# Two attention loops written out in a fixed order on four engines, in a two-layer hybrid encoder

## The chip, the core and the metric

The kernel runs on one core of one Trainium2 chip. The core has a matrix engine (TensorE, PE in the profile, with its weight loads shown as PEld), a vector engine (VectorE, DVE), a scalar engine (ScalarE, ACT), a general engine (GpSimd, POOL) and an engine that here only issues transfers (SyncE, SP). Each engine takes its own instructions strictly in order; between engines they wait on semaphores. The metric is the device time of one execution in microseconds (us), lower is better. A result is the median of several executions; the profile is that of one more execution.

## The reference

The input is 512 tokens of 1024 numbers, all float32, laid out as a grid of 8 by 64. Two layers are computed, and each is `h = h + attention(rmsnorm(h))` followed by `h = h + mlp(rmsnorm(h))`; a last rmsnorm gives the output.

```python
# layer 0: two groups of heads beside each other, one input and one output projection
qa, ka, va, cq, ckv, kr = split(h @ w_in)
qa = axial_rope(rmsnorm(qa), row, col)        # A: 8 query heads, 2 key/value heads of 64
ka = axial_rope(rmsnorm(ka), row, col)
oa = softmax(qa @ ka.T / 8) @ va
qb = rmsnorm(cq) @ b_w_uq                     # B: 8 heads from latents of 384 and 256
kvb = rmsnorm(ckv) @ b_w_ukv                  # 64 plain + 32 rotary, the rotary key shared
ob = softmax([q_nope, rope(q_rope)] @ [k_nope, rope(kr)].T / sqrt(96)) @ vb
h = h + concat(oa, ob) @ w_out
# layer 1: 16 heads, each query sees a clamped window of 8 rows by 16 columns
h = h + softmax(q @ k_window.T / 8 + bias) @ v_window @ w_out
# after either: square of relu
h = h + relu(rmsnorm(h) @ w_up) ** 2 @ w_down # 1024 -> 4096 -> 1024
```

## The kernel before, in words

**Numbers.** Every float32 operand of a matrix product is kept as a pair: a rounded part `hi` (a copy on ACT into the type fp32r) and the rest `lo` (a subtract, mostly on DVE, some on POOL). A product is three matmuls, hi by hi, hi by lo and lo by hi (`mm3`, L425 to L428). So each piece of data costs a copy on ACT and a second half on DVE before PE can use all of it. `split` (L741 to L743) does this for activations, `chunk` (L172 to L204) for weights, which a transfer on SP brings in as `raw` first. `weights(i)` (L217) makes chunks two ahead of their use.

**Filler.** Products that are not urgent are generators. `Fill` (L391 on) holds a queue of them; `fill.run(us)` adds credit and emits groups of three matmuls until it is used up. A group is booked at `MM3` = 0.69 us. The attention loops call `step` after each unit of work and so put filler between the units.

**Layer 0.** After the first projections, the filler queue gets the latents of q and kv (cq, ckv), the rotary key (`rotary_key`), the scales of the latents (`latents`), and the q, k and v parts of B's first four heads (`projB(0)`). Then `attend` (L851 on) goes over 16 heads (A's eight, then B's two groups of four) and 4 blocks of 128 queries, 64 units in all. For a unit, `scores` (L892) makes the score matmuls (L895), a reduce on DVE that scales, writes the scores to memory and takes the least (L899), the exp on ACT with its sum (L901), the reciprocal on DVE (L902) and the norm by it on POOL (L903). `transpose` (L856) takes the unit three back: four PE transposes (L862), a copy on ACT (L864) and a subtract on DVE (L865). `values` (L870) follows for each two units (L875), and at a head's end the two halves of the accumulator are added (L884, L885). At unit 35 the filler queue gets the output projection of the first four head pairs and `projB(1)`. `step` runs 1.5 us of filler per unit.

A's queries for head pairs 1 to 3 are rotated inside the loop: `rope_q` starts eight transfers on SP for the swapped rows and a multiply by cos on POOL (L486), and also emits the multiply by sin on POOL (L487); `sum_q` (L545 on) adds both on DVE (L547), splits the result and lays it out with three transfers on SP. It is called two units after `rope_q`.

**Layer 1.** `attend_C` (L1233 on) goes over 16 heads of 4 units in three steps: scores of units 3 and 0 (L1248), then `second` (transposes, L1271, and evacuation, L1275 and L1276, of the head before), filler; `finish` (values) of the head before, scores of units 1 and 2, filler; first transposes of this head, filler. `weigh` (L1250 on) is reduce (L1254), exp (L1256), reciprocal (L1257) and norm on POOL (L1258). The filler is the q/k projection of the next head pair (`projC`) and the values' (`valuesC`). `projC` lays out keys by three transfers of 256 KB for each head pair, issued from POOL's queue (L1186 twice, then L1187, which waits until the lo and hi parts are made and for what it overwrites). `step` runs 3.4, 2.85 or 4.0 us of filler, by the head.

**What sets the order.** The program names the operations in the order of the code above, and a scheduler then decides the order on each engine by its own estimates. The MLPs, with seven products in place of eight for most blocks, are outside the change.

Of the kernel before, what the change touches and what calls it, by code (L numbers as in the profile page):

```python
# [18 lines left out]
P = 128  # L19
# [16 lines left out]
def encoder_kernel(ctx: ExitStack, tc: tile.TileContext, ins, out, dbg=None):  # L36
# [136 lines left out]
    def chunk(parts, nk, ncol, heads=None, eng=None, first=False):  # L173
# [13 lines left out]
        v = lambda t: t[:, 0:m].rearrange("p (k n) -> p k n", k=nk)  # L187
        if heads is None:
# [4 lines left out]
            (eng or DVE).tensor_tensor(lo_[:, 0:m], raw[:, 0:m], f32(hi[:, 0:m]), op=ALU.subtract)  # L193
        else:

            na, nb = heads
            hn = ncol // (na + nb)
            r4 = r3.rearrange("p k (h e) -> p k h e", h=hn)
            for e0, n, o in ((0, na, 0), (na, nb, hn * na)):
                z = [v(t)[:, :, o : o + hn * n].rearrange("p k (h e) -> p k h e", h=hn) for t in (hi, lo_)]  # L200
                src = r4[:, :, :, e0 : e0 + n]
                ACT.activation(z[0], src, AF.Copy)
                (eng or DVE).tensor_tensor(z[1], src, f32(z[0]), op=ALU.subtract)
        return v(hi), v(lo_)  # L204
# [5 lines left out]
    asked, ready = [], []  # L210
# [18 lines left out]
    def seven_chunk(w, k0, c0):  # L229
# [10 lines left out]
        DVE.tensor_tensor(lo[:, 0:896], raw[:, 128:1024], f32(hi[:, 0:896]), op=ALU.subtract)  # L240
        return hi, lo
# [154 lines left out]
    class Fill:  # L396
# [33 lines left out]
    def split_g(src, g, dst):  # L430

        ACT.activation(dst[:, 0, :], src, AF.Copy, scale=g)
        DVE.scalar_tensor_tensor(dst[:, 1, :], src, g, f32(dst[:, 0, :]), op0=ALU.mult, op1=ALU.subtract)
# [42 lines left out]
    def rope(src, cos, sin, mask, n=P, far=False):  # L476

        sh = scratch()
        if far:
            q = mask[0]  # L480
            for b in range(0, n, q):
                SP.dma_start(sh[b : b + q, :], src[b ^ q : (b ^ q) + q, :])
        else:
# [3 lines left out]
        (POOL if far else DVE).tensor_tensor(sh[0:n, :], sh[0:n, :], sin[0:n, :], op=ALU.mult)  # L487
        if far:
            return c, sh
        DVE.tensor_tensor(c[0:n, :], c[0:n, :], sh[0:n, :], op=ALU.add)  # L490
        return c

    def stats_to_tok(bk, n, name):

        st = scratch()
        ACT.activation(st[0:n, :], bk[0:n, :], AF.Copy)
        tb = stb()
# [45 lines left out]

    def sum_q(t):
# [5 lines left out]
        DVE.tensor_tensor(lo, rt, f32(q[:, 0, :]), op=ALU.subtract)  # L550
        SP.dma_start(f32(q[0:64, 1, :]), f32(q[64:128, 0, :]))
        SP.dma_start(f32(q[64:128, 1, :]), f32(lo[64:128, :]))
        SP.dma_start(f32(q[64:128, 0, :]), f32(lo[0:64, :]))
# [81 lines left out]
    def load_w(k):  # L635
        W[k] = chunk([(0, 768, rows(w_in, k, 1)[:, :, 0:768])], 1, 768, first=k == 0)
# [54 lines left out]
    def ev_kr(b):  # L691
        kc, kl = scratch(), scratch()
        ACT.activation(kl[0:32, :], b[32:64, :], AF.Copy)
        DVE.tensor_tensor(kc[0:32, :], b[0:32, :], kl[0:32, :], op=ALU.add)
        kr = rope(kc, cosB, sinB, sw8, 32)
        bk = stb()
        bcast_cols(lambda i: r0[:, i : i + 1].to_broadcast([P, 32]), 32, bk)
        DVE.tensor_tensor(kr[0:32, :], kr[0:32, :], bk[0:32, :], op=ALU.mult)
        kp = kst.pair()
        ACT.activation(kp[0:32, 0, :], kr[0:32, :], AF.Copy)  # L700
        DVE.tensor_tensor(kp[0:32, 1, :], kr[0:32, :], f32(kp[0:32, 0, :]), op=ALU.subtract)

    def rotary_key():
# [13 lines left out]
        w.free()  # L717
        ev_kr(b)

    def latents():  # L720

        b = stb()
        for z in range(2):
            PE.matmul(b[0:2, :], ind2(z), sqs[z].t[:, 0:512], start=z == 0, stop=z == 1)
        sB = stats_to_tok(b, 2, "rsB")
        for z in range(2):
            sqs[z].free()
        scB = keep([P, 4], F32, "scB")
        DVE.tensor_scalar(scB, sB[:, :, 0], -(96.0 ** -0.5), 1.0, op0=ALU.mult, op1=ALU.mult)
        bk = stb()  # L730
        bcast_cols(lambda i: sB[:, i, 1:2].to_broadcast([P, P]), P, bk)
        hold["skvb"] = Slot(F32)
        ACT.activation(hold["skvb"].t[:, 0:512], bk, AF.Copy)
        hold["sB"], hold["scB"] = sB, scB
        for s_ in X:
            s_.free()
        yield 1.5
# [3 lines left out]
    def split(src, dst):  # L741
        ACT.activation(dst[:, 0, :], src, AF.Copy)
        DVE.tensor_tensor(dst[:, 1, :], src, f32(dst[:, 0, :]), op=ALU.subtract)  # L743
# [3 lines left out]
    def projB(g, last):  # L747
# [5 lines left out]
        def q_part():  # L753
            CQ = [s_.pair() for s_ in cqS]
            banks = three(3)
            for m in (2, 0, 1):
                for k in range(3):
                    hi, lo = (z[:, k % 2, m * P : (m + 1) * P] for z in weights(iq[k // 2]))
                    mm3(banks[m], hi, lo, CQ[k][:, 0, :], CQ[k][:, 1, :], k == 0, k == 2)
                    yield MM3  # L760
                if m == 2:
                    qc = scratch()
                    ACT.activation(qc, banks[2], AF.Copy)
                    qr = rope(qc, cosB, sinB, sw8)
                    stg = Slot()
                    split(qr, stg.pair())
                else:
# [3 lines left out]
                    split(banks[m], qa)  # L771
                    SP.dma_start(f32(qb[0:64, :, :]), f32(qa[64:128, :, :]))
                    for e, q in enumerate((qa, qb)):
                        j = 2 * m + e
                        SP.dma_start(f32(q[64:96, :, :]), f32(stg.pair()[32 * j : 32 * j + 32, :, :]))
# [5 lines left out]
        def k_part():  # L781
            CK = [s_.pair() for s_ in ckS]
            banks = three(2)
            for m in range(2):
# [8 lines left out]
                split(kn, ka)  # L793
                SP.dma_start(f32(kb[0:64, :, :]), f32(ka[64:128, :, :]))
                for k_ in (ka, kb):
                    SP.dma_start(f32(k_[64:96, :, :]), f32(kst.pair()[0:32, :, :]))
# [5 lines left out]
        def v_part():  # L802
# [3 lines left out]
            for ip in range(2):  # L806
# [13 lines left out]
                for ii in range(2):  # L820
# [3 lines left out]
                    DVE.scalar_tensor_tensor(v[:, ii, :, 64:128], src, sB[:, i, 1:2], f32(v[:, ii, :, 0:64]),  # L824
                                             op0=ALU.mult, op1=ALU.subtract)
# [4 lines left out]
        fill.add(f"q{g}", q_part())  # L830
# [18 lines left out]
    O = []  # L849

    def attend(heads, step):  # L851
# [17 lines left out]
        def values(h, half, pt):  # L869
# [9 lines left out]
            if half:  # L879
                a = 64 * h["e"]  # L880
                if h["e"] == 0:
                    hold["pair"] = scratch()
                c = scratch()
                ACT.activation(c[0:64, :], o[64:128, :], AF.Copy)  # L884
                DVE.tensor_tensor(hold["pair"][a : a + 64, :], o[0:64, :], c[0:64, :], op=ALU.add)  # L885
                if h["e"]:
                    O.append(Slot())
                    split(hold["pair"], O[-1].pair())
                h["after"]()

        def scores(h, i):
# [9 lines left out]
            ACT.activation(p, p, AF.Exp, bias=t[:, 1:2], scale=-1.0, accum_out=t[:, 2:3])  # L901
            DVE.reciprocal(t[:, 3:4], t[:, 2:3])  # L902
            POOL.tensor_scalar(p, p, t[:, 3:4], 1.0, op0=ALU.mult, op1=ALU.mult)  # L903
            return p

        for h in heads:
            for i in range(4):
                ripe = list(late_v)
                p = scores(h, i)
                if len(late_t) == 3:  # L910
                    transpose(*late_t.pop(0))
                late_t.append((h, i, p))
                if ripe:
                    values(*late_v.pop(0))
                step(h, i)
        for x in late_t:
# [3 lines left out]
            fill.run(1.5)  # L920

    def heads_A():
        for h in range(8):
# [17 lines left out]
    def heads_B(g):  # L941
        fill.until(f"v{g}")
        Q, K, V = (QKV[g][z] for z in "QKV")
        vv = [s_.t.rearrange("p (i h e) -> p i h e", i=2, h=4) for s_ in V]
        for j in range(4):
# [12 lines left out]
            def after(j=j):  # L958
                if j == 3:
                    for s_ in V:  # L960
# [3 lines left out]
                       vlhs=lambda kt, j=j: vv[kt // 2][:, kt % 2, j, :])  # L964

    rate = {"A": 1.5, 0: 1.5, 1: 0.75}
# [8 lines left out]
    def step(h, i):  # L975
        n = count[0]
        count[0] += 1
        if n == 35:

            ok = [s_.pair() for s_ in O]  # L980
            assert len(ok) == 4
            out_proj(w_out, 0, ok, [0, 1, 2], "out")
            projB(1, True)
            out_proj(w_out, 0, ok, [3, 4, 5], "out")
# [540 lines left out]
```

## Time and profile before

| | us |
|---|---|
| median of 3 runs | 1211.41 |
| lowest and highest | 1211.27, 1213.22 |
| the profiled execution, its own time | 1211.92 |
| the span of its profile | 1210.0 |
| first loop, first score matmuls to last values | about 67 to 250 |
| second loop | about 652 to 839 |

The span goes from the first to the last instruction that the profile shows; 1.92 us of the execution lie around it. In the profile a line number is a line of the kernel before, busy times are sums over an engine's instructions, and the shown length of a matmul includes time in which the next one already runs. The granted clock (PEclk) is the share of TensorE's full speed. The two MLPs fill 264 to 640 and most of 840 to 1210 us.

### The profile page before, as it was taken

To read this page: it belongs to the slowest core of one execution; us is meant where nothing else is said; L and a number is where in the kernel's file an instruction comes from. 1 tells how busy PE (TensorE), PEld (TensorE's weight loads), DVE (VectorE), ACT (ScalarE), POOL (GpSimd) and SP (SyncE) were. 2 spreads that over 40 slices of the span, in tenths; PEclk is the share of its full clock that TensorE was granted. 3 is DMA by queue.
4 is the path that set the end of the run, shared out by engine and by line. 5 is a ranking of instruction groups with operands and counts; after the bars stand their busy time and mean duration, and the time that the engine had idled before them with its cause. 6 is when DMAs were issued, how large, how long until landed. Compare 5 with 4: busy or idle time off the path is not lost.

```text
span 1210.0 us, 18784 instructions
## 1 busy us (share of the span) xinstructions
PE 1182.8 (98%) x6804; PEld 1012.4 (84%) x6804; DVE 797.6 (66%) x1409; ACT 615.0 (51%) x1035; POOL 424.5 (35%) x543
## 2 busy tenths in 40 slices
PE   9998999999999999999999999999999999999997
PEld 8676888887899889898887988988778988988985
DVE  4587888878678337547565666666984753764764
ACT  5577676764346326336434555554463642451553
POOL 3256252205365146146002122321244803713800
PEclk9999999999999999999999999999999999999999
DMA  7223214212234214347435454443222341351432
GB/s 241 71 66 93 74 49 132 70 53 70 79 88 148 87 61 131 96 124 232 129 87 157 140 152 132 126 114 106 70 79 61 106 157 44 88 158 44 122 122 70
DMA packets 105853, 127.96 MB, mean 106 GB/s; under 512 B 8755, under 2 KB 77664, under 8 KB 105760
## 3 DMA queue, kind: packets, MB, share of 16 engines
q1 hardware_dynamic: 102832, 119.30, 33.4%
q0 software_dynamic: 2176, 6.31, 2.2%
q10 hardware_dynamic: 752, 1.15, 0.3%
q8 instruction: 54, 0.88, 0.3%
q14 instruction: 39, 0.32, 0.1%
HBM read 104.32 MB, written 6.29 MB: 91 GB/s over the span
## 4 chain that ended last, share of the span: by engine, by line
PE 81%; DVE 8%; ACT 3%; POOL 3%; issue 2%; DMA 1%; SPq 1%; DVEq 0%; POOLq 0%; ACTq 0%
PE mm L428 7%; PE mm L427 7%; PE mm L426 7%; PE s L428 2%; PE s L426 2%; PE s L427 2%; PE o L875 2%; PE s L895 2%; PE mm L316 2%; PE mm L314 2%; PE mm L315 2%; PE mm L1424 2%; PE mm L1425 2%; PE mm L1423 2%; PE t L862 2%
## 5 line engine op out<-in xcount | busy, mean ns | idle before, releaser
L193 DVE TENSOR_TENSOR wlo<-raw,whi 128x1024 fp32r<-128x1024 f32 (+2 forms) x133 | 157.4, 1185 | 156.5 <-ACT whi L192 153.3
L192 ACT ACTIVATE whi<-raw 128x1024 fp32r<-128x1024 f32 (+2 forms) x136 | 134.7, 993 | 172.0 <-PE o L427 38.7
L240 DVE TENSOR_TENSOR wlo<-raw,whi 128x896 fp32r<-128x896 f32 x104 | 129.7, 1247 | 107.2 <-ACT whi L239 105.7
L426 PE MATMUL mm<-a,whi 128*128 128x512 f32 x460 | 185.6, 406 | 0.1
L427 PE MATMUL mm<-a,whi 128*128 128x512 f32 x460 | 183.1, 398 | 0.1
L428 PE MATMUL mm<-a,wlo 128*128 128x512 f32 x460 | 182.0, 397 | 0.1
L239 ACT ACTIVATE whi<-raw 128x896 fp32r<-128x896 f32 x104 | 98.8, 950 | 161.6 <-POOL raw L236 27.7
L234 POOL TENSOR_TENSOR raw<-raw 128x128 f32<-128x128 f32 x104 | 60.0, 577 | 266.7 <-DMA raw<-in_ffn_w_up_dram 190.3
L428 PEld LDWEIGHTS mm<-a,wlo 128*128 128x128 f32 x460 | 86.6, 189 | 21.1 <-issue 1.7
L427 PEld LDWEIGHTS mm<-a,whi 128*128 128x128 f32 x460 | 87.1, 189 | 18.9 <-issue 1.7
L426 PEld LDWEIGHTS mm<-a,whi 128*128 128x128 f32 x460 | 86.8, 189 | 18.4 <-issue 1.0
L235 POOL TENSOR_TENSOR raw<-raw 128x256 f32<-128x256 f32 x104 | 95.3, 917 | 8.2
L236 POOL TENSOR_TENSOR raw<-raw 128x128 f32<-128x128 f32 x104 | 92.4, 888 | 8.1
L316 PE MATMUL mm<-a,wlo 128*128 128x256 f32 x280 | 79.3, 283 | 1.8 <-DVE wlo L240 1.6
L315 PE MATMUL mm<-a,whi 128*128 128x256 f32 x280 | 78.6, 281 | 0.0
L314 PE MATMUL mm<-a,whi 128*128 128x256 f32 x280 | 78.6, 281 | 0.0
L903 POOL TENSOR_SCALAR p<-p,ti 128x512 f32<-128x512 f32 x64 | 45.6, 714 | 89.3 <-DVE ti L902 79.5
L1258 POOL TENSOR_SCALAR p<-p,ti 128x256 f32<-128x256 f32 x64 | 37.1, 584 | 110.4 <-DVE ti L1257 103.8
L316 PEld LDWEIGHTS mm<-a,wlo 128*128 128x128 f32 x280 | 52.7, 188 | 3.0 <-DVE wlo L240 2.8
L314 PE MATMUL t<-a,whi 128*128 128x256 f32 x192 | 53.9, 281 | 0.0
L315 PE MATMUL t<-a,whi 128*128 128x256 f32 x192 | 53.8, 280 | 0.0
L316 PE MATMUL t<-a,wlo 128*128 128x256 f32 x192 | 53.8, 280 | 0.0
(318 smaller groups left out, 3186.4 us busy)
## 6 DMA issues: line engine op xcount, KB each, us to landing
raw<-in_ffn_w_down_dram SPq DMA_DIRECT2D x64, 512.0 KB
raw<-in_ffn_w_up_dram SPq DMA_DIRECT2D x104, 256.0 KB
raw<-in_od_w_qkv_dram SPq DMA_DIRECT2D x64, 128.0 KB
raw<-in_ffn_w_up_dram SPq DMA_DIRECT2D x12, 512.0 KB
a<-a POOLq DMA_DIRECT2D x24, 256.0 KB, 3.8
raw<-in_ev_w_in_dram SPq DMA_DIRECT2D x12, 384.0 KB
bias<-bx SPq DMA_DIRECT2D x16, 256.0 KB
raw<-in_od_w_qkv_dram SPq DMA_DIRECT2D x8, 512.0 KB
```

The lines of the kernel that those rows point to most:

```text
L192: ACT.activation(hi[:, 0:m], raw[:, 0:m], AF.Copy)
L193: (eng or DVE).tensor_tensor(lo_[:, 0:m], raw[:, 0:m], f32(hi[:, 0:m]), op=ALU.subtract)
L235: POOL.tensor_tensor(r[:, 4:6], r[:, 2:3].to_broadcast([P, 2, P]), r[:, 0:7:6], op=ALU.add)
L236: POOL.tensor_tensor(r[:, 7], r[:, 3], r[:, 5], op=ALU.subtract)
L239: ACT.activation(hi[:, 0:896], raw[:, 128:1024], AF.Copy)
L240: DVE.tensor_tensor(lo[:, 0:896], raw[:, 128:1024], f32(hi[:, 0:896]), op=ALU.subtract)
L314: PE.matmul(o, wh, x[:, 0], start=kp == 0 and z == 0, stop=False, skip_group_check=True)
L315: PE.matmul(o, wh, x[:, 1], start=False, stop=False, skip_group_check=True)
L316: PE.matmul(o, wl, x[:, 0], start=False, stop=kp == self.np - 1, skip_group_check=True)
L426: PE.matmul(o, wh, xh, start=first, stop=False)
L427: PE.matmul(o, wh, xl, start=False, stop=False)
L428: PE.matmul(o, wl, xh, start=False, stop=last)
```

## The change

Both loops are wrapped in `fixed_order()`, a region in which PE, ACT, DVE and POOL run in the order in which the program emits the instructions. SP is still scheduled. Filler of `LEAD` = 8.0 us is emitted first in each region. Inside a region:

- A unit's reciprocal and norm are emitted after the next unit's reduce (`norm(*last)`); the transposes three back come ahead of the exp. In the second loop the exps, the reciprocals and the norms of two units are put apart by parts of the filler.
- `soon` puts second halves off (lo subtracts, the add of the accumulator's halves in `fold`, the add of `rope`, and the transfers that depend on them); `catch_up` emits them in the next unit. `chunk` returns its lo subtract, and `give_low` emits it one chunk behind.
- Filler per unit is 1.15 us in the first loop; in the second 2.85 us a step, 3.6 from head 13, cut in parts of 0.4 and 0.6 in two of the three steps.
- The sin multiply of a rotary query goes into a step of its own (`sin_q`, third unit of the pair's first head) and `sum_q` two units later.
- `latents` becomes three pieces that run beside the q part of B's first group; heads of B wait for the k part and, when the values need it, the v part. At unit 35 `projB(1)` stands ahead of the whole output projection.
- The 24 key transfers of the second loop go to SP's queue, after the put-off subtract. The rotary rows of B's queries go to their places at the end of the q part.

The diff, cut to its core:

```diff
-            (eng or DVE).tensor_tensor(lo_[:, 0:m], raw[:, 0:m], f32(hi[:, 0:m]), op=ALU.subtract)
+            low(lo_[:, 0:m], raw[:, 0:m], hi[:, 0:m])
...
-    def weights(i):
-        while len(ready) < min(i + AHEAD + 1, len(asked)):
+    def weights(i, ahead=AHEAD):
+        while len(ready) < min(i + ahead + 1, len(asked)):
             make, spec = asked[len(ready)]
-            ready.append(make(*spec))
+            hi, lo, lows = make(*spec)
+            ready.append((hi, lo))
+            low_parts.append(lows)
+
+            give_low(len(ready) - fixed[0])
+        give_low(i + 1)
         return ready[i]
+    put_off = []
+
+    def soon(z):
+        if fixed[0]:
+            put_off.append(z)
+        else:
+            z()
+
+    def catch_up():
+        todo, put_off[:] = list(put_off), []
+        for z in todo:
+            z()
...
     def split(src, dst, then=lambda: None):
+        def low():
+            DVE.tensor_tensor(dst[:, 1, :], src, f32(dst[:, 0, :]), op=ALU.subtract)
+            then()
+
         ACT.activation(dst[:, 0, :], src, AF.Copy)
-        DVE.tensor_tensor(dst[:, 1, :], src, f32(dst[:, 0, :]), op=ALU.subtract)
+        soon(low)
...
+    def fixed_order():
+        return tc.manual_schedule(engines={mybir.EngineType.PE, mybir.EngineType.Activation, mybir.EngineType.DVE,
+                                           mybir.EngineType.Pool})
...
         for h in heads:
             for i in range(4):
                 ripe = list(late_v)
-                p = scores(h, i)
+                p, t = scores(h, i)
+                if last:
+                    norm(*last)
+                catch_up()
                 if len(late_t) == 3:
                     transpose(*late_t.pop(0))
+                ACT.activation(p, p, AF.Exp, bias=t[:, 1:2], scale=-1.0, accum_out=t[:, 2:3])
+                last = p, t
                 late_t.append((h, i, p))
                 if ripe:
                     values(*late_v.pop(0))
                 step(h, i)
...
-                if e == 0 and t < 3 and i == 2:
-                    sum_q(t + 1)
+                if t < 3 and (e, i) in ((0, 2), (1, 0)):
+                    if e:
+                        sum_q(t + 1)
+                    else:
+                        sin_q()
...
-        fill.run(1.5)
+        fill.run(1.15)
...
-    attend(all_heads(), step)
-    fill.until("out")
+    with fixed_order():
+        fixed[0] = 1
+        fill.run(LEAD)
+        attend(all_heads(), step)
+        fill.until("out")
+        finish_off()
+        give_low(len(ready))
+        fixed[0] = 0
...
-                split(n_, ka)
-                for z in range(2):
-                    POOL.dma_start(f32(kb[64 * z : 64 * z + 64, :, :]), f32(ka[64:128, :, :]))
-                POOL.dma_start(f32(ka[64:128, :, :]), f32(ka[0:64, :, :]))
+                def lay_out():
+                    for z in range(2):
+                        SP.dma_start(f32(kb[64 * z : 64 * z + 64, :, :]), f32(ka[64:128, :, :]))
+                    SP.dma_start(f32(ka[64:128, :, :]), f32(ka[0:64, :, :]))
+
+                split(n_, ka, lay_out)
...
-            scores(h, (3, 0))
+            w = scores(h, (3, 0))
+            catch_up()
             if late[0]:
                 second(late[0])
-            step(n, 0)
+            for x in w:
+                weigh(*x)
+            step(n, 0, 0.4)
+            for x in w:
+                norm(*x)
+            step(n, 0, 0.6)
...
-        fill.run(3.4 if n < 4 else 2.85 if n < 13 else 4.0)
+        fill.run((2.85 if n < 13 else 3.6) * part)
```

More of the change, by code (lines that the diff above doesn't have):

```diff
@@ L202, in chunk @@
                 ACT.activation(z[0], src, AF.Copy)
-                (eng or DVE).tensor_tensor(z[1], src, f32(z[0]), op=ALU.subtract)
-        return v(hi), v(lo_)
+                low(z[1], src, z[0])
+        return v(hi), v(lo_), lows
     def rows(w, k0, nk):
         return w[k0 * P : (k0 + nk) * P, :].rearrange("(k p) n -> p k n", p=P)
-    asked, ready = [], []
+    asked, ready, low_parts = [], [], []
     AHEAD = 2
@@ L486, in rope, with add @@
         POOL.tensor_tensor(c[0:n, :], src[0:n, :], cos[0:n, :], op=ALU.mult)
[L487 to L490, printed above, removed]
+        DVE.tensor_tensor(sh[0:n, :], sh[0:n, :], sin[0:n, :], op=ALU.mult)
+        def add():
+            DVE.tensor_tensor(c[0:n, :], c[0:n, :], sh[0:n, :], op=ALU.add)
+            if then:
+                then(c)
+        soon(add)
         return c
@@ L693, in ev_kr, with add, end @@
         ACT.activation(kl[0:32, :], b[32:64, :], AF.Copy)
[L694 to L701, printed above, removed]
+        def add():
+            DVE.tensor_tensor(kc[0:32, :], b[0:32, :], kl[0:32, :], op=ALU.add)
+            rope(kc, cosB, sinB, sw8, 32, then=end)
+        def end(kr):
+            bk = stb()
+            bcast_cols(lambda i: r0[:, i : i + 1].to_broadcast([P, 32]), 32, bk)
+            DVE.tensor_tensor(kr[0:32, :], kr[0:32, :], bk[0:32, :], op=ALU.mult)
+            kp = kst.pair()
+            ACT.activation(kp[0:32, 0, :], kr[0:32, :], AF.Copy)
+            soon(lambda: DVE.tensor_tensor(kp[0:32, 1, :], kr[0:32, :], f32(kp[0:32, 0, :]), op=ALU.subtract))
+        soon(add)
     def rotary_key():
@@ L828, in v_part @@
                     s_.free()
-        fill.add(f"q{g}", q_part())
+        fill.add(f"q{g}", q_part() if last else beside(q_part(), latents()))
         fill.add(f"k{g}", k_part())
@@ L879, in values @@
             if half:
[L880 to L888, printed above, removed]
+                fold(o, h["e"])
                 h["after"]()
@@ L915, in attend @@
                 step(h, i)
+        norm(*last)
         for x in late_t:
@@ L1350, in encoder_kernel, with step @@
     w_out1 = ins["od_w_out"][0]
-    def step(n, z):
-        if n == 13 and z == 0:
+    def step(n, z, part):
+        if n == 13 and z == 0 and part < 0.5:
+            finish_off()
             for s_ in X:
@@ L1359, in step @@
                 out_proj(w_out1, 0, ok, cols, "out")
-        fill.run(3.4 if n < 4 else 2.85 if n < 13 else 4.0)
-    attend_C(step)
-    fill.until("out")
+        fill.run((2.85 if n < 13 else 3.6) * part)
+    with fixed_order():
+        fixed[0] = 1
+        fill.run(LEAD)
+        attend_C(step)
+        fill.until("out")
+        finish_off()
+        give_low(len(ready))
+        fixed[0] = 0
     ok = [s_.pair() for s_ in O[6:]]
```

220 lines of the change are left out of this document (142 added, 78 removed).

## The prediction

> **What bounds the kernel now.** I read the page's busy line first, then the busy time of each engine by stretches of the span, then the chain of waits inside the stretches where TensorE (PE) is not full.
>
> ```profile
> span 1210.0 us, 18784 instructions
> PE 1182.8 (98%) x6804; PEld 1012.4 (84%) x6804; DVE 797.6 (66%) x1409; ACT 615.0 (51%) x1035; POOL 424.5 (35%) x543
> ```
>
> PE is the bound of the whole, and the change gives it the same matmuls. Only time in which PE waits can be won: 1210.0 - 1182.8 = 27.2 us by this line. The next view splits it. Columns: from:to, length, then busy us of PE, PEld, DVE, ACT, POOL, and the granted PE clock.
>
> ```profile
> 48.00:68.00 20.00, 19.42 (x77) 11.45 (x76) 13.26 (x35) 11.40 (x22) 3.86 (x3) 1.00 0.32 83
> 68.00:115.00 47.00, 41.89 (x235) 33.39 (x234) 36.06 (x95) 37.53 (x82) 31.64 (x35) 1.00 0.27 76
> 115.00:160.00 45.00, 44.48 (x246) 34.92 (x247) 39.04 (x100) 29.82 (x65) 14.77 (x18) 0.96 0.30 73
> 160.00:250.00 90.00, 89.72 (x531) 75.58 (x530) 76.15 (x174) 62.46 (x132) 29.07 (x39) 1.00 0.29 81
> 250.00:264.00 14.00, 14.00 (x62) 11.18 (x62) 11.12 (x16) 8.84 (x13) 0.00 (x0) 1.00 0.14 39
> 650.00:690.00 40.00, 37.59 (x247) 32.96 (x246) 25.88 (x74) 22.39 (x54) 11.43 (x22) 1.00 0.55 153
> 690.00:810.00 120.00, 116.89 (x722) 102.75 (x721) 77.33 (x209) 66.82 (x151) 31.99 (x56) 1.00 0.49 132
> 810.00:840.00 30.00, 29.78 (x156) 24.82 (x155) 18.41 (x45) 14.09 (x31) 4.90 (x8) 1.00 0.39 111
> ```
>
> Two loops are in reach: the first (48 to 250 us, 64 units of one head and 128 queries) and the second (650 to 840, 16 heads of 4 units). PE is idle for 0.58 + 5.11 + 0.52 + 0.28 = 6.5 us in the first and 2.41 + 3.11 + 0.22 = 5.7 us in the second. That is a floor, because a matmul's shown length is longer than its turn:
>
> ```profile
> 48.62 0.39 PE L428 MATMUL mm<-a,wlo 128*128 128x512 f32 x1
> 48.85 0.40 PE L426 MATMUL mm<-a,whi 128*128 128x512 f32 x1
> ...
> 51.37 0.43 DVE L577 COPY sc<-rsA 128x512 f32<-128x512 f32 x1
> ...
> 51.85 0.33 PE L454 MATMUL t<-cst,sc 128*128 128x128 f32 x1
> ```
>
> The two starts are 0.23 us apart and each lasts 0.40, so the first 0.17 us of any stall leaves no idle time. If each of 64 units hides one such stall, the first loop loses up to 64 x 0.17 = 11 us more, and the second, in 48 steps, up to 8 us (an estimate from that overlap). Now the large gaps, from finer stretches:
>
> ```profile
> 64.00:68.00 4.00, 3.45 (x15) 2.52 (x14) 3.13 (x10) 1.78 (x3) 1.29 (x1) 1.00 0.27 77
> 96.00:100.00 4.00, 2.55 (x16) 1.96 (x16) 3.94 (x11) 3.90 (x9) 1.72 (x2) 1.00 0.43 116
> 112.00:116.00 4.00, 1.43 (x9) 1.06 (x9) 2.22 (x5) 2.36 (x6) 2.44 (x3) 0.97 0.00 0
> 116.00:120.00 4.00, 3.93 (x15) 2.44 (x15) 3.70 (x8) 2.98 (x7) 1.97 (x2) 0.61 0.76 180
> 650.00:654.00 4.00, 2.42 (x15) 1.87 (x14) 2.54 (x5) 1.74 (x3) 0.00 (x0) 1.00 0.64 166
> 700.00:704.00 4.00, 2.40 (x12) 1.68 (x11) 3.73 (x9) 2.63 (x7) 1.86 (x1) 1.00 0.35 101
> ```
>
> The gap of 2.57 us at 112 is paid twice: in the next 4 us the clock is 0.61, which loses 4 x 0.39 = 1.56 us. The chain names its cause:
>
> ```profile
> 107.99 3.27 DMA raw<-in_ev_b_w_uq_dram
> 111.26 1.27 POOL a L621
> 112.53 1.23 POOL sc L487
> ...
> 115.19 1.01 PE o L875 x5
> ```
>
> A weight load queued on SP behind eight rotary copies holds POOL; the rotary multiply L487 (sin) follows on POOL, a DVE add waits for that, and the lo half that the values matmuls (L875) need sits behind the add.
>
> **The change, part by part.** The written order puts sin one or two units ahead of the add that needs it and sends filler of 1.15 us instead of 1.5 us per unit, so that it lasts to the end.
>
> *Entry of the first loop, +3.4 us.* The written region is emitted behind everything before it, so on PE only one filler group (three matmuls) now stands ahead of the transposes L454, where five stood. Their input, the copy L577, does not come earlier: it ends at 51.80. The group's third matmul is the one at 48.62, its turn ends at 48.85, and PE starts again at 51.85: 3.0 us idle, with every later matmul behind it. From that I take the 0.55 us of idle at 64:68, which the 8 us of filler (12 groups of 0.69) put ahead of the first scores covers: +2.4. For the clock, the gap at 112 says up to 1.56 us behind a gap of this size; PE would also wait part of that time for a bank that ACT empties, so I take +1.0. Bounds 0 and +4.0.
>
> The Trainium skill, page "TensorE: Matmul & The Clock Gate", section "What's actually happening", says that the clock halves after an idle window of about 3.4 us. By that neither gap would suffice and the clock term is nothing (total 1202.5); the row at 116:120 speaks against it, and the row decides.
>
> *Units 0 to 19 (68 to 120 us), -7.8 us.* The sin multiply no longer precedes the subtracts of its own unit, and second halves go one unit later, behind the reduce. The waits at 96, 100 to 104 and 112 have their inputs a unit earlier. All idle of 68:115 goes, 5.1, with the clock loss, 1.56 and 4 x 0.03 = 0.12, and about six hidden starts of 0.17, 1.0: -7.8. Bounds -7.8 and 0. What is late next is the reciprocal, which waits one unit for its exp and so finds it done.
>
> *Units 20 to 34, +3.0 us.* Here DVE is nearly full: 39.04 of 45 us. Filler falls by 0.35 us a unit, so 15 units give PE 5.3 us less cover while DVE keeps its work (rotary key, latents, the splits of q and k): 45 - 5.3 = 39.7 us of PE against 39.04 of DVE that must now go in one fixed order with its waits. Bounds 0 (DVE is ahead by its slack of units 0 to 19) and +5.3 (all the missing cover shows as idle). I take +3.0, nearer to the upper end, since a 39.04 of 39.7 leaves no room for a wait.
>
> *Units 35 to 63, -2.0 us.* 160:250 shows 0.28 idle and up to 29 x 0.17 = 4.9 hidden; the 35 x 0.35 = 12 us of filler kept back comes into units that had none. Bounds -5.2 and 0. The rotary q copies of the second head group go to the end of their part on SP and its heads wait for k instead of v: nothing, since 160:250 shows no wait on them, and a late one would cost its landing, 3.27 us by the row at 107.99. At the exit nothing: 250:264 is full at 14.00, and the next products interleave as before.
>
> First loop: 3.4 - 7.8 + 3.0 - 2.0 = -3.4 us.
>
> *Second loop, entry and K, -1.5 us.* The chain there:
>
> ```profile
> 652.63 1.16 PE s L1248 x8
> ...
> 660.31 3.83 DMA a<-a
> ...
> 664.69 3.04 DMA a<-a
> ```
>
> K is laid out by three 256 KB copies a head pair, the third after the first has landed. Twelve filler groups (8 us) before the first scores cover the wait at 650:654 (1.58 us); its K still needs two transfers of some 3.8 us in a row, about 8 us, so I take 1.0 of it, and 0.5 of 656 to 668. Bounds -2.5 and 0. All 24 copies move from POOL to SP:
>
> ```profile
> POOL a L1186 <- DVE a L743: 85.0, 4, 77.4
> POOL a L1187 <- DMA a<-a: 21.9, 7, 4.8
> ```
>
> (waits in us: total, times, longest). POOL loses those waits; SP gains eight of up to 4.8 us, and the weight, bias and Q loads queue behind them. Weights are asked two chunks ahead and a pair's copies come once in two heads, so I take 0; the other end is that all seven waits, 21.9 us, pass on to PE.
>
> *Second loop, steps, -3.5 us.* The large gap at 700:704:
>
> ```profile
> 701.04 0.49 ACT L1256 ACTIVATE p<-p,ti 128x256 f32<-128x256 f32 x1
> ...
> 701.44 0.18 ACT L1256 ACTIVATION_READ_ACCUMULATOR p<-p,ti 128x1 f32 x1
> ...
> 701.81 0.16 DVE L1257 RECIPROCAL ti<-ti 128x1 f32<-128x1 f32 x1
> 701.89 1.21 DVE L193 TENSOR_TENSOR wlo<-raw,whi 128x1024 fp32r<-128x1024 f32 x1
> ...
> 702.14 2.34 POOL L1258 TENSOR_SCALAR p<-p,ti 128x256 f32<-128x256 f32 x2 [4.71 <-DVE ti L1257]
> ...
> 704.08 0.33 PE L1271 MATMUL t<-cst,p 128*128 128x128 f32 x1 [1.68 <-POOL p L1258]
> ```
>
> and, in the chain of waits,
>
> ```profile
> 702.14 1.89 POOL p L1258
> ```
>
> The two norms on POOL took 2.34 us, the first 1.89, so the second 0.45; the first ran beside the 1.21 us weight subtract. In the changed order the weight subtracts of nearly all heads stand behind both reciprocals and behind the evacuation that follows. The idle of 690:840, 3.33, goes but for 0.3; 2.0 of the 8 hidden goes; +1.5 comes in head 0, where a subtract of 1.21 us does stand ahead of the reciprocals: -3.5. Bounds -11 and +1.5.
>
> Sum: 1211.92 - 3.4 - 1.5 - 3.5 = **1203.5 us** against the profiled execution's own time (span 1210.0 plus 1.92 around it, which stays). The median of the runs lies 0.5 lower, 1211.41; I forecast 1203.
>
> **Rivals.**
>
> *Slower: the norm late in the second loop, 1217.* From the reduce's end to the transposes: exp 0.49 + 0.18, reciprocal 0.16, norm 0.45, three hand-overs of 0.1: 1.6 us for one unit, covered by 2.85 us of filler. A weight subtract ahead of the reciprocal (1.21) and one beside the norm (1.89 - 0.45 = 1.44) make it 4.2, late by 1.4. Where a weight chunk ends on that step, taken as 7 of 16 heads, that is 7 x 1.4 = 10 us, and the steps win nothing: 1211.9 - 3.4 - 1.5 + 10 = 1217. It decides from four heads on (5.6 us against the 4.9 won elsewhere). For it: the row of 1.89. Against it: the order named above.
>
> The Trainium skill, page "GPSIMD Engine Reference", section "1. Specifications", has POOL share its memory interface with VectorE and contend with instructions of two SBUF inputs. The trace agrees: 1.89 us beside such a subtract, 0.45 without.
>
> *No change in the first loop, 1208.* DVE becomes the bound of units 20 to 34 (+5.3), the clock drops in full (+1.56), the end wins nothing: 2.4 + 1.6 - 7.8 + 5.3 = +1.5, and the second loop -5.0: 1211.9 + 1.5 - 5.0. For it: 39.04 of 45. Against it: DVE comes with slack out of units 0 to 19, 36.06 of 47.
>
> *All the lost time comes back, 1194.* Entry 2.4 without the clock, -7.8, 0, -3.5 makes -8.9; the second loop 5.7 visible and 3 hidden, -8.7. Against it: the fixed order cannot fill a gap with what is ready.
>
> *It does not do what it says, 1211.* SP stays scheduled, and its late loads set the order anyway.
>
> **How the numbers follow.** Forecast (1197 to 1207) 0.46; slower rival 0.16; no change in the first loop (1207 to 1212) 0.19; all back 0.13; not what it says 0.06. Within 0.2% (2.4 us) is about what a measurement of this kernel cannot tell from no change. Faster by more, under 1209: 0.46 + 0.13 + half of 0.19 = 0.68; within: half of 0.19, less a little, and 0.06 = 0.14; slower 0.18. The range reaches from the all-back case to the slower rival's lesser half: 1193 to 1216.
>
> **What would show it.** Right: PE waits about 3 us near 49 with a clock under 1 soon after; no gap over 1 us from 68 to 120; small gaps at 125 to 160; the wait at 650 under 1 us; POOL norms all near 0.45 in the second loop. Wrong: SP copies waiting while weight loads arrive late, norms of over 1 us before transposes, or DVE over 95% in 120 to 160 with PE waiting on it.

## The result, and the profile after

The changed kernel takes 1259.44 us (median of 4 runs, 1257.84 to 1260.36) against 1212.24 before: a ratio of 1.0388, 95% interval 1.037 to 1.0406. It is 47 us slower where 8 us faster was forecast, and far outside the range.

The busy line of the page after the change, with its span:

```profile
span 1256.8 us, 18733 instructions
PE 1195.1 (95%) x6804; PEld 1018.2 (81%) x6804; DVE 798.7 (64%) x1409; ACT 615.3 (49%) x1035; POOL 412.3 (33%) x519
```

The span is 46.8 us longer. PE is idle for 1256.8 - 1195.1 = 61.7 us in place of 27.2, so 34.5 us are new waits. The other 12.3 us are longer matmuls: the same 6804 are busy for 1195.1 us in place of 1182.8. The granted clock is 0.986 over the whole in place of 0.995. The busy time of DVE and ACT is the same to 1.1 us, and POOL's is 12.2 us lower. So no engine got more to do.

Where it was lost shows in the stretches (columns as before: busy PE, PEld, DVE, ACT, POOL, clock):

```profile
48.00:68.00 20.00, 16.96 (x61) 9.13 (x60) 12.68 (x39) 11.69 (x21) 2.55 (x2) 0.91 0.26 66
68.00:115.00 47.00, 41.79 (x233) 34.42 (x231) 34.36 (x82) 34.49 (x75) 29.24 (x31) 1.00 0.28 74
115.00:160.00 45.00, 37.17 (x188) 27.84 (x189) 32.06 (x82) 22.50 (x47) 16.34 (x18) 0.89 0.23 54
160.00:250.00 90.00, 76.31 (x426) 62.68 (x425) 62.91 (x147) 54.50 (x119) 26.11 (x34) 0.96 0.24 66
...
676.00:700.00 24.00, 19.23 (x95) 15.52 (x93) 9.67 (x29) 8.46 (x20) 2.79 (x6) 1.00 0.54 133
700.00:800.00 100.00, 97.04 (x621) 85.88 (x620) 63.88 (x174) 55.52 (x128) 19.79 (x34) 1.00 0.52 142
800.00:850.00 50.00, 41.07 (x242) 34.92 (x242) 25.86 (x75) 22.54 (x56) 6.57 (x14) 0.90 0.36 97
```

From 115 to 160 us PE falls from 44.48 to 37.17 busy, and DVE from 39.04 to 32.06, ACT from 29.82 to 22.50 with it. Three engines are idle more at the same time. That points to a chain of waits, and not to a full engine. The first score matmul of the second loop starts at 683.0 us in place of 652.6, and its last one at 875.6 in place of 830.1:

```profile
L1386 PE MATMUL s<-a,a x128: 274/281/561, 683.0 to 875.6; 128*128 128x256 f32 x128
```

```profile
L1248 PE MATMUL s<-a,a x128: 276/281/387, 652.6 to 830.1; 128*128 128x256 f32 x128
```

So 30.4 us are lost up to the second loop, 15.1 more in it, and 1.3 after it.

What PE waits for in the first loop (us in total, times, longest), from the view of waits after the change:

```profile
PE o L990 <- DVE a L980: 5.8, 11, 1.2
PE mm L781 <- DVE a L777: 3.8, 1, 3.8
PE mm L466 <- POOL wlo L191: 3.5, 3, 2.1
PE mm L464 <- ACT whi L207: 3.2, 1, 3.2
PE t L977 <- DVE a L980: 2.2, 1, 2.2
PE t L802 <- DVE a L980: 2.1, 1, 2.1
PE t L977 <- DVE sc L763: 2.0, 1, 2.0
```

There is no one cause. The first row is eleven short waits of the values for their lo halves. The others are one wait each, three for L466, and most are 2 to 4 us long. They are for different things: the rotary key's weight (L781), the second latent projection's weight (L464, L466), and one of the two result banks `t` that DVE has not yet read. That last wait holds the sums for the latents' scales (L802) and the transposes (L977), behind a unit's subtract (L980) or the rotary key (L763).

The longest single wait, in the timeline:

```profile
107.32 4.99 SPq L522 DMA_DIRECT2D sc<-a  x8
...
112.41 0.52 SPq L775 DMA_DIRECT2D sc<-in_ev_w_in_dram  x1
...
115.03 0.42 ACT L776 ACTIVATE a<-sc 128x256 fp32r<-128x256 f32 x1 [1.39 <-DMA sc<-in_ev_w_in_dram]
115.48 0.43 DVE L777 TENSOR_TENSOR a<-sc,a 128x256 fp32r<-128x256 f32 x1 [1.05 <-ACT a L776]
115.97 1.54 PE L781 MATMUL mm<-a,a 128*64 128x512 f32 x3 [3.76 <-DVE a L777]
```

The eight rotary copies take SP 4.99 us to issue, and the weight of the rotary key stands behind them in SP's queue. Before the change the same eight copies held another load and PE lost 2.57 us at the same time of the run. The wait did not go; it now holds another operation, and at 3.76 us it is longer.

### The profile page after: what moved, and what is told of

The parts are those of the page before. It is cut to its first block, busy times and chain, and to the rows that moved or that the text cites. A ratio compares the mean times of both kernels' runs of the same rounds, so it can differ in the third digit from the quotient of the medians.

```text
span 1256.8 us, 18733 instructions
## 1 busy us (share of the span) xinstructions
PE 1195.1 (95%) x6804; PEld 1018.2 (81%) x6804; DVE 798.7 (64%) x1409; ACT 615.3 (49%) x1035; POOL 412.3 (33%) x519
## 3 DMA queue, kind: packets, MB, share of 16 engines
q10 hardware_dynamic: 752, 1.15, 0.3%
## 5 line engine op out<-in xcount | busy, mean ns | idle before, releaser
L464 PE MATMUL mm<-a,whi 128*128 128x512 f32 x460 | 188.3, 411 | 8.3 <-ACT whi L207 3.2
L466 PE MATMUL mm<-a,wlo 128*128 128x512 f32 x460 | 184.0, 401 | 6.1 <-POOL wlo L191 3.5
L466 PEld LDWEIGHTS mm<-a,wlo 128*128 128x128 f32 x460 | 87.5, 190 | 30.7 <-POOL wlo L191 4.8
L464 PEld LDWEIGHTS mm<-a,whi 128*128 128x128 f32 x460 | 87.6, 191 | 29.6 <-issue 5.5
L979 ACT ACTIVATE a<-t 128x512 fp32r<-128x512 f32 x64 | 37.9, 594 | 43.2 <-PE t L977 41.3
```

Source lines behind the costliest of these rows:

```text
L464: PE.matmul(o, wh, xh, start=first, stop=False)
L466: PE.matmul(o, wl, xh, start=False, stop=last)
```

## The experiments

Every kernel below is the changed one with the edit shown. Theory 1 was that the fixed order costs: in it an engine that comes to a late input stands, with ready work behind it. Theory 2 was that the other edits cost.

**Which loop.** The regions are taken away from both loops, from the second, or from the first:

```diff
-    with fixed_order():
+    with ExitStack():
```

> The changed kernel with every edit, but both loops left to the scheduler. Theory 1 (the fixed order itself costs: an engine stands still at a late input with ready work behind it): most of the 47 us comes back, 1205 to 1220. Theory 2 (the other edits cost: filler of 1.15, second halves put off, key copies on SP): it stays above 1245. Theory 1's chance as I see it: 0.7.

> The changed kernel with the fixed order in the first loop only. In the two profiles the second loop's first score matmul starts 30.4 us later after the change (683.0 against 652.6) and its last one 45.6 later, so the second loop's own share is 15.2. Theory 1: 1259 less about 15, so 1240 to 1248. Theory 2: 1255 to 1260, no change.

> The changed kernel with the fixed order in the second loop only. Theory 1: 1259 less about 30, so 1222 to 1234. Theory 2: 1255 to 1260. The two halves should add up: what this run and the run with the first loop alone fixed win over the changed kernel, together about the whole difference to the run with none fixed.

With both loops scheduled: **1202.96 us** (1201.12 to 1206.48), ratio to before 0.9937 (0.9916 to 0.9959). First loop fixed: 1237.28, ratio 1.0215 (1.02 to 1.0231). Second loop fixed: 1224.45, ratio 1.0111 (1.0094 to 1.0128). Theory 2 is out: all other edits together win some 8 us where the scheduler sets the order. The fixed order costs 34.3 us in the first loop and 21.5 in the second, 55.8 together, and 56.5 when both are fixed. Both are more than the 30.4 and 15.1 us that the trace had shown, since that counted the loss against the kernel before and not against the better scheduled one. So the run with the first loop fixed came out under its expected range, and so did the run with neither fixed; the run with the second loop fixed lies in its range.

The stretch from 775 to 810 us, second loop fixed and then neither fixed:

```profile
775.00:810.00 35.00, 26.13 (x140) 21.07 (x140) 19.09 (x57) 16.81 (x43) 4.97 (x11) 0.87 0.30 76
...
800.00:805.00 5.00, 2.68 (x12) 2.12 (x12) 2.15 (x9) 2.16 (x6) 1.72 (x4) 0.61 0.66 157
805.00:810.00 5.00, 2.62 (x7) 1.62 (x6) 3.63 (x10) 3.76 (x8) 0.23 (x1) 0.50 0.28 62
```

```profile
775.00:810.00 35.00, 33.42 (x178) 27.70 (x177) 23.23 (x65) 18.74 (x47) 10.03 (x14) 1.00 0.37 106
```

PE is idle for 7.3 us more in these 35 us. A lower clock costs only while PE is busy: 2.68 x 0.39 and 2.62 x 0.50, some 2.4 us. Together that is nearly half of the second loop's 21.5. Another 4.2 us of idle lie at the loop's entry, where 640:660 has PE busy for 15.49 us in place of 19.66. The timeline of the kernel with the second loop fixed shows how such a wait is made:

```profile
797.29 0.50 ACT L1397 ACTIVATE p<-p,ti 128x256 f32<-128x256 f32 x1
...
797.48 0.68 DVE L1316 TENSOR_TENSOR sc<-mm,rb 128x512 f32<-128x512 f32 x1
...
798.20 0.63 ACT L830 ACTIVATE a<-sc 128x512 fp32r<-128x512 f32 x1 [0.31 <-DVE sc L1316]
...
798.86 0.69 DVE L827 TENSOR_TENSOR a<-sc,a 128x512 fp32r<-128x512 f32 x1 [0.70 <-ACT a L830]
799.47 0.22 DVE L1400 RECIPROCAL ti<-ti 128x1 f32<-128x1 f32 x2
...
799.82 0.94 POOL L1401 TENSOR_SCALAR p<-p,ti 128x256 f32<-128x256 f32 x2 [8.39 <-DVE ti L1400]
...
800.35 0.94 PE L1412 MATMUL t<-cst,p 128*128 128x128 f32 x3 [1.65 <-POOL p L1401]
```

The second exp ends at 797.79. The two reciprocals take 0.22 us and could run at 798.16, when DVE is done with L1316. But on DVE they stand behind L827, which waits 0.70 us for a copy on ACT (L830). DVE stands, and the reciprocals, the norms and the transposes with it; PE waits 1.65 us and has nothing else that its order lets it do.

**Which engine.** The set of engines in the region is cut:

```diff
-        return tc.manual_schedule(engines={mybir.EngineType.PE, mybir.EngineType.Activation, mybir.EngineType.DVE,
-                                           mybir.EngineType.Pool})
+        return tc.manual_schedule(engines={mybir.EngineType.PE})
```

> The changed kernel with the fixed order on PE alone; ACT, DVE and POOL left to the scheduler, both loops. All four fixed cost 56 us against none fixed (1259.4 against 1203.0). Theory P (PE itself stands at a late operand while ready filler waits behind it, so PE's order is the cost): 1240 to 1260. Theory Q (ACT, DVE and POOL make the operands late by standing in their own order, and PE only shows it): 1203 to 1218.

> The changed kernel with the fixed order on ACT, DVE and POOL, PE left to the scheduler. Theory P: 1203 to 1215, since PE can pass a late operand. Theory Q: 1235 to 1260.

> The changed kernel with the fixed order on DVE alone. DVE is the fullest of the three (39.1 of 45 us from 115 to 160 before). Theory Q with DVE as the engine: 1220 to 1250. Theory P: under 1212.

> The changed kernel with the fixed order on ACT and POOL alone. In its trace with all four fixed, PE waits 3.2 us for a weight's hi part on ACT and 3.5 us for lo parts on POOL, all for the second latent projection, so 6.7 us and the clock behind them: 1205 to 1215 by either theory; above 1225 would say that these two engines' order makes operands late far beyond the waits that name them.

| engines in fixed order | us | ratio to before (95%) | above none fixed |
|---|---|---|---|
| none | 1202.96 | 0.9937 (0.9916 to 0.9959) | 0 |
| DVE | 1208.32 | 0.9985 (0.9976 to 0.9995) | 5.4 |
| ACT, POOL | 1219.77 | 1.0077 (1.0062 to 1.0092) | 16.8 |
| ACT, DVE, POOL | 1226.55 | 1.0132 (1.0117 to 1.0147) | 23.6 |
| PE | 1229.13 | 1.0151 (1.0134 to 1.0168) | 26.2 |
| all four | 1259.44 | 1.0388 (1.037 to 1.0406) | 56.5 |

The runs come from three rounds, in which the kernel before took 1209.89 to 1212.24 us, so the last column is good to some 2 us.

Neither P nor Q holds alone: PE's order costs about half, that of the other three the other half, and the halves add up to 49.8 of 56.5. DVE, the fullest of the three and the one on which I had looked for the cost, costs the least of the sets that were run. ACT and POOL, which were not run apart, cost 16.8 us against the 6.7 us of waits that name them. That lies between the two halves of the expectation, over 1215 and under 1225. With PE alone fixed, two waits stand out, 11.0 us together, in a profile of the longest of its five executions (1234.93 us):

```profile
PE mm L781 <- DVE a L777: 6.6, 1, 6.6
PE t L493 <- DVE rsB L556: 4.4, 1, 4.4
```

**Which input.** Six kernels kept all four engines fixed and took single causes away. First the filler of the first loop back to the amount before (`fill.run(1.5)`), and the weights' lo subtracts no longer one chunk behind (`give_low(len(ready))`):

> The changed kernel with filler of 1.5 us instead of 1.15 per unit of the first loop. Theory A (the filler is booked too thin, and values wait on their lo halves where units have little of it): up to 6 us faster, 1250 to 1257. Theory B (units 30 to 34 have no filler in either case because the queue holds 43 us of it at 0.69 a group and runs dry; more per unit makes it dry from unit 24 on): slower by 3 to 12 us, 1262 to 1271.

> The changed kernel, four engines fixed, with a weight chunk's lo subtract emitted with the chunk and not one chunk behind. In its trace PE waits 3.5 us for lo parts on POOL and 1.1 on DVE in the first loop, and some 3 in the second, with the clock lower behind them. If the delay by one chunk is what makes these late: 1246 to 1254. Rival: the subtract then stands ahead of the loop's own work on DVE and POOL, and those waits move to the norms and the values: 1257 to 1265.

1259.86 us (ratio 1.0402, 1.0386 to 1.0418) and 1259.18 (1.0393, 1.0373 to 1.0412). Neither moves anything. The first fits neither half of its expectation; the second lies where the rival of its expectation put it.

Then the late inputs made early: the rotary key's weight is loaded and split before the loop, and the chunks of `projB(1)` are asked for behind those of `projB(0)`:

```diff
+        return key_rest(w, w4)
+
+    def key_rest(w, w4):
+
         b = mmb()
...
+    PB = [plansB(0), plansB(1)]
     projB(0, False)
```

> The changed kernel, four engines fixed, with the rotary key's weight loaded and split before the loop, and the weights of the second latent projection asked for right behind those of the first. This takes away the input of three waits that its trace shows: 3.8 us for the rotary key's weight, 3.2 for the hi part, about 3.5 for lo parts, 10.5 in all, and 2 to 4 us of lower clock behind them: 1245 to 1250 if waits go one by one. Rival: in a fixed order the next late input takes their place at once: 1253 to 1259.

1246.74 us, ratio 1.0295 (1.0278 to 1.0312): 12.7 us won, or 11.3 by the two ratios, against 10.5 us of waits and 2 to 4 of clock expected. By the two profiles PE is idle for 52.0 us in place of 61.7, and its matmuls are busy for 3.8 us less. Some 1.4 of these 3.8 are the entry, where the clock in 52:56 was 1.00 this time and not 0.64. So a late input costs its wait, and 2 us or so of the clock behind the waits came back with them.

Then the filler queue. By its bookings it holds 43.1 us in the first loop and 111.4 in the second. With 8 us emitted ahead it runs dry after 30 units (8 + 30 x 1.15) and 36 steps (8 + 36 x 2.85), which is in units 30 to 34 and in head 12:

```diff
-        fill.run(1.15)
+        fill.run(1.0 if n < 35 else 1.15)
...
-        fill.run((2.85 if n < 13 else 3.6) * part)
+        fill.run((2.65 if n < 13 else 3.6) * part)
```

> The changed kernel, four engines fixed, with filler per unit so that the queue lasts: 1.0 us in place of 1.15 up to unit 35 (8 + 35 x 1.0 = 43, the queue holds 43.1 us), and 2.65 a step in place of 2.85 up to head 13 (8 + 39 x 2.65 = 111, the queue holds 111.4). If the dry queue is the cause of the waits in units 30 to 34 (about 6 us) and from 775 to 810 (7.3 us idle and 4.5 of lower clock): 1244 to 1250. If those waits only move to where the filler is thinner: 1255 to 1261.

1259.80 us, ratio 1.0413 (1.0393 to 1.0433). The rival holds: the waits moved. Slower filler makes the k part of B late, and the first scores of B now wait for a transfer:

```profile
PE s L1002 <- DMA a<-a: 5.8, 1, 5.8
```

with the clock at 0.83 from 160 to 200 us. Then the norms of the second loop directly behind the exps, ahead of the filler:

```diff
-            step(n, 0, 0.4)
             for x in w:
                 norm(*x)
-            step(n, 0, 0.6)
+            step(n, 0, 1.0)
```

> The changed kernel, four engines fixed, with the second loop's reciprocals and norms emitted directly behind the exps, ahead of the step's filler and what that puts on DVE. In its trace the transposes wait 8.8 us for the norm on POOL, the longest 2.2 in the first head, where the reciprocals stand behind three chained operations and a weight subtract on DVE. If that order is the cause: 1247 to 1253, with the clock behind it. Rival: DVE now stands waiting for the exps, and the filler's own halves come late instead: 1257 to 1262.

1257.84 us, ratio 1.04 (1.0379 to 1.0421). The 2.2 us in the first head went, and the rest of the expected gain did not come: 7.4 us of waits for the norm remain where 8.8 were, in other heads, one of them 4.3 us long. The time is again the rival's. At last the early inputs, the slower filler and the earlier norms together, with the 8 us of filler ahead of the regions:

> The changed kernel, four engines fixed, with the early inputs, the lasting queue and the earlier norms together, and with the 8 us of filler emitted ahead of each fixed region, so that PE does not stand at the transposes before the first loop (3.0 us and a clock of 0.91 in 48:68). If the causes named are the whole of the cost and add up: 1259 - 12.7 - 11 - 9 - 5 = 1217 to 1225. If a fixed order always meets another late input: 1230 to 1245. At the scheduled time of 1203 only if nothing else stands.

1248.45 us, ratio 1.0316 (1.0297 to 1.0334). The causes do not add up: this is no better than the early inputs alone. It misses even the pessimistic half of the expectation. It also carries the slower filler, and with it a wait of 6.5 us for B's first scores; the other cures without the slower filler were not run together. So it is shown that the waits moved, and not that every cure must uncover another late input.

**What the rest of the change wins.** Five more kernels left both loops to the scheduler, each with one thing undone or added: the rotary key's weight loaded before the loop; the key copies of the second loop back on POOL; nothing put off (`fixed[0] = 0`); the filler's amounts as before (`fill.run(1.5)`, and 3.4, 2.85 and 4.0 a step); the slower filler of the diff above.

> The changed kernel with both loops left to the scheduler, and the rotary key's weight loaded and split before the loop. With the scheduler PE still waits 2.1 us for that weight at 114. If the wait goes: 1199 to 1201.5, against 1203.0. If another input was as late: 1202 to 1204.

> The changed kernel with both loops left to the scheduler, and the 24 key copies of the second loop issued from POOL as before. If the move to SP is what wins in the second loop (its last score matmul comes 5.3 us earlier than before the change, counted from its first loop's end): 1206 to 1209. If the copies' queue does not matter: 1201 to 1204.

> The changed kernel with both loops left to the scheduler and nothing put off (second halves and weight subtracts are named at once). The scheduler orders by readiness, so the place where an operation is named should matter little: 1201 to 1206. If the put-off is what wins the 8 us against the kernel before: 1208 to 1212.

> The changed kernel with both loops left to the scheduler and the filler per unit as in the kernel before (1.5 us in the first loop; 3.4, 2.85 and 4.0 a step in the second, in the same parts). If the spread of the filler is what wins: 1208 to 1212, as before. If it is what else moved (the order in which scores, reciprocals, transposes and the latents' pieces are named): 1202 to 1206.

> The changed kernel with both loops left to the scheduler and filler of 1.0 us per unit to unit 35 and 2.65 a step to head 13, so that the queue lasts. With the scheduler, PE's gaps over 1 us are 3.3 us in all from 90 to 115, 1.4 from 130 to 160 and 2.8 from 740 to 820: if thin filler at the queue's end causes the last two, 1199 to 1202; if not, 1202 to 1206.

They take 1204.25 (ratio 0.9949, 0.9933 to 0.9965), 1204.02 (0.9942, 0.9928 to 0.9956), 1206.16 (0.9961, 0.9946 to 0.9977), 1204.53 (0.9947, 0.9933 to 0.9961) and 1205.76 (0.9953, 0.9938 to 0.9969). All beat the kernel before, by less than 1%, and their intervals overlap with one another and with that of 0.9937. So 5 to 8 us are won by what all of them share, and none of the five things tried carries all of it. What does is not settled: the order in which a unit's operations are named, the sin multiply's new place and the latents in pieces were not tried by themselves. The fastest version is the change without its fixed order, 1202.96 us; it beats both kernels.

## Why the prediction was wrong, step by step

- **Entry of the first loop, +3.4.** Right in its place and size. In 48:52 PE is busy for 1.17 of 4 us, and in 52:56 the clock is 0.64, or 1.4 us. The same gap (2.8 us of shown idle, 3.0 with the 0.17 hidden) stands in eight traces: that of the changed kernel and those of seven kernels above that fix PE in the first loop. The clock fell behind it in four of them (0.50 to 0.64 from 52 to 56) and stayed at 1.00 in four:

```profile
48.00:52.00 4.00, 1.17 (x9) 0.73 (x8) 3.12 (x10) 1.54 (x3) 0.00 (x0) 1.00 0.39 104
52.00:56.00 4.00, 3.80 (x12) 1.72 (x11) 2.59 (x5) 3.15 (x7) 0.87 (x1) 0.64 0.25 65
```

```profile
48.00:52.00 4.00, 1.16 (x7) 0.65 (x5) 3.28 (x11) 1.90 (x4) 0.00 (x0) 1.00 0.36 99
52.00:56.00 4.00, 3.29 (x15) 1.64 (x14) 2.41 (x4) 2.81 (x6) 0.53 (x1) 1.00 0.19 52
```

  The first pair is the changed kernel, the second the one with early inputs. So 1.0 was a fair middle, and that this run came near it is luck. By the idle window of about 3.4 us that the Trainium skill states (page "TensorE: Matmul & The Clock Gate", section "What's actually happening") a gap of 3.0 us would do nothing; in four of eight traces it did.
- **Units 0 to 19, -7.8.** Wrong, and nothing was won: 68:115 idles 5.21 us in place of 5.11. The step that failed reads "All idle of 68:115 goes". I followed the sin multiply, the wait's last link, and did not ask what held it first: SP's eight copies, which the change leaves where they were. Behind them the rotary key's weight was late, by 3.76 us, and 116:120 has a clock of 0.50 in place of 0.61.
- **Units 20 to 34, +3.0.** Wrong in mechanism and size. 115:160 idles 7.83 us in place of 0.52 and loses up to 5.0 (45 x 0.11) to the clock in place of 1.8 (45 x 0.04), so some 10 us. The first 1.0 of the idle is the end of the wait at 112, and part of the clock lies behind that wait too; the rest comes after it. I had DVE nearly full and bounded the cost by the filler that is missing. DVE was busy 32.06 of 45 us. The cost was not a full engine but engines that waited for each other in turn, and the bound of 5.3, which counts missing filler, does not cover that.
- **Units 35 to 63, -2.0.** Wrong in sign. 160:250 idles 13.69 us in place of 0.28. I took the spread filler for a gain and did not look at its weights: `projB(1)` is planned at unit 35, so its hi and lo parts stand in the fixed order of ACT and POOL close ahead of their use. In the profile before the change nothing waits for these lo parts (L203). In the timeline after it:

```profile
180.41 2.47 ACT L207 ACTIVATE whi<-raw 128x512 fp32r<-128x512 f32 x6
180.54 0.69 DVE L827 TENSOR_TENSOR a<-sc,a 128x512 fp32r<-128x512 f32 x1 [0.70 <-ACT a L830]
181.11 3.07 POOL L191 TENSOR_TENSOR wlo<-raw,whi 128x512 fp32r<-128x512 f32 x4 [2.52 <-ACT whi L207]
181.39 0.50 PE L464 MATMUL mm<-a,whi 128*128 128x512 f32 x1 [3.24 <-ACT whi L207]
```

- **Second loop, entry and K, -1.5.** Wrong: PE waits 2.6 us before the first scores, where 1.58 were idle before. The profile names nothing for this wait. SP issued the last key copy at 680.12, 2.9 us before these scores at 683.0, so I take it for that copy's landing, which is inferred. That the copies' queue is worth nothing was right where the scheduler sets the order (1204.02 with POOL, 1202.96 with SP); with the fixed order it was not run.
- **Second loop, steps, -3.5.** The +1.5 for head 0 was right in its place (2.2 us). The rest was wrong: 800:850 idles 8.93 us, and from 835 to 845 PE is busy for 6.3 us at a clock of 0.50, another 3.2. Over the loop the waits for the norm come to 8.8 us in eight places; where I followed one, the reciprocals stood behind other waiting work on DVE. A weight's hi part on ACT adds 2.4. I had checked that no weight subtract stands ahead of them and had not checked what else on DVE waits there.
- **The rivals.** The slower one named the right wait, transposes that wait for the norm. Of its reasons, a slow POOL was not the main one: the median norm takes 0.48 us in the changed kernel as before, the longest 1.45. A reciprocal behind other work on DVE was near what happened. That its 10 us lie near the 8.8 of these waits is luck, since it priced weight subtracts. The last rival named SP's late loads, and priced them at no loss. No rival covered the first loop's 30.4, so the range had no room for it. This is the step that failed over all: "the fixed order cannot fill a gap with what is ready" stood only against the best case, and the sum has no term for it. It should have been a rival with a price on every engine; it cost 56.5 us.

Shown is that this fixed order costs 56.5 us against the same program scheduled, that PE's order, DVE's, and ACT's with POOL's each have a share, and that three late inputs gave back about their waits when they were made early. Not shown is a short list of causes behind it: the six attempts to make one brought 0, 0, 12.7, 0, 1.6 (inside its interval) and 11.0 us.

## What to carry to other kernels

When the order on several in-order engines is written by hand, ask at every instruction that can wait what is queued behind it, on each engine and on the queue that stays scheduled; a sum of busy times and slack says nothing about that. A wait that is traced to its last link is not removed by moving that link: follow it to the queue where it begins. And keep the edits apart from the mechanism that carries them: here the edits win some 8 us and the fixed order loses 56, which one run without the region shows.

## What the runs showed of the hardware that I had not expected

The granted clock behind a gap on PE is not settled by the gap's length. The gap before the first loop, 2.8 us of idle, was followed by 0.50 to 0.64 in four executions and by 1.00 in four. A gap of 2.1 us at 114 in the scheduled kernel was followed by 1.00, and one of 2.57 us before the change by 0.61. Over the whole kernel this is no small thing: of the 46.8 us, 12.3 are the same matmuls running longer. Against the scheduled version it is 18.4 of 57.5 us (PE busy 1195.1 and 1176.7, spans 1256.8 and 1199.3).
